# First product of a one-core transformer block: modulation columns through a product with ones, the high part of h taken from PSUM, halved first weights, another order of loads, filler products

## The chip, the core and the metric

The kernel runs on one NeuronCore of a Trainium2 chip. The metric is the device time of one execution in microseconds (us); lower is better. Five engines work side by side: TensorE (PE, matrix products; PEld is its weight load), VectorE (DVE), ScalarE (ACT), GpSimd (POOL) and SyncE (SP), which here only issues DMA transfers. All five run their own instructions strictly in the order in which the program lists them and wait for each other through semaphores.

## The reference

One layer of a hybrid block on 256 tokens of width 2048, all in float32:

```python
mod = silu(c) @ w_ada + b_ada                 # 6 x 2048: shift1, scale1, gate1, shift2, scale2, gate2
h = rms_norm(x, norm1_w) * (1 + scale1) + shift1
proj = h @ w_in                               # columns of an mLSTM group and an attention group
...                                           # mLSTM (4 heads), differential attention (8 heads)
x = x + gate1 * (concat(h_ml, o_da) @ w_out)
h = rms_norm(x, norm2_w) * (1 + scale2) + shift2
g, u = split(h @ w_gate_up)
x = x + gate2 * ((silu(g) * u) @ w_down)
```

So nothing of the first projection can start before a part of `mod` is known: for each pair of 128-row blocks of the model width, `shift1` and `scale1` of those rows. One such pair is called p (0 to 7).

## The kernel before

**Ticks.** The main stream of PE is a list of ticks. A tick multiplies 256 rows of K by 512 output columns for all 256 tokens. A float32 operand is split in a high part of type float32r and a low part (the rest), and three products stand for one: high by high, weight-low by h-high, weight-high by h-low (lines 568 to 570, `product`). A tick has 12 such products of 128x512. Its names are `wh` and `wl` (weights, high and low), `hh` and `hl` (activations), `acc('in', g, p)` (the accumulator in PSUM; `in` is the first projection, `wo` the output projection). `r` is the raw weight tile as it lands; there are three of them. ACT makes `wh` (line 211, helper `act`), DVE makes `wl` (line 181, helper `tt`), two ticks ahead of PE.

**Modulation.** `w_ada` comes in quarters of 0.5 MB (`ada`, four buffers). Some pairs are done on PE (`on_pe`): four quarters are multiplied into `gv` (line 216, 4 instructions a quarter, 8 in the trace), ACT copies `gv` to `gr`, PE transposes `gr` in two blocks into `gc` (line 220), and ACT copies four of the columns to `gsum`. POOL then adds the bias and the four parts (lines 376 and 378) and forms `gcol` = (1 + scale) x norm weight (lines 416 and 417). The other pairs are summed by DVE straight from `ada` (line 185).

**From x to h.** ACT scales x to `hx`, PE transposes it into `pt`, ACT applies `gcol` and the shift from `pt` into `hx` (128x256 twice), ACT copies that to `hh`, DVE subtracts to get `hl`.

**The order of work.** There is no scheduler: the order in the code is the order on each engine. Before the ticks stands a prelude written by hand. In the ticks, a planner (`Plan`) places steps of background work (the later h pairs, gates, attention heads, mLSTM cells) between half ticks, by estimated costs and by free PSUM banks. So an edit early in the program can move such steps much later. The background work that the text below speaks of: `gt` (the gate projection with the small weights `gwt`, line 216 from `project_gates`), `sc` (attention scores of one head, with `bmask`/`identb` products in bf16 between them), `ot` (transposes of the attention output of one group, whose high and low parts are `odh` and `odl`, inputs of the output projection), `nu`, `pp` and `L` (mLSTM), `g1rp` (spreading of the gate row).

**Loads.** All loads stand in one queue on SP. A load waits there until its buffer is free; everything behind it waits too. `small` holds the gate weights (64 KB, line 1268) and the lambda parameters.

Of the kernel before, what the change touches and what calls it, by code (L numbers as in the profile page):

```python
# [56 lines left out]
FPAIRS = 6  # L57
FSWEEPS = ((0, 2), (2, 5), (5, 8))
# [22 lines left out]
class Work:  # L81
    """Background work in steps; a step follows the one before it by at least a tick."""
# [7 lines left out]
class Plan:  # L90
    """Interleaves the steps of background work with the ticks of the main matrix products."""
# [73 lines left out]
def tile_block(ctx, tc, x, c, pos, par, w_ada, w_in, w_gt, w_out, w_gu, w_dn, out):  # L165
# [103 lines left out]
    gsum = const([P, 6, 4, 16], "gsum")  # L269
# [51 lines left out]
    def ada_use():  # L321
        s, p, q = items[ada_next[1]]
        t = ada_tiles.pop((s, p, q))
        if on_pe(s, p):
            if q == 0:
                assert plan.free > 0, "no bank"
                plan.free -= 1
                gemv[s, p] = misc(f"gv{s}_{p}")
            pg = gemv[s, p]
            for j in range(4):  # L330
                mm(pg[32 * j:32 * j + 32, :256], scol[:, q * 4 + j, :], t[:, j * 256:(j + 1) * 256], q == 0, q == 3,
                   passes=1.2, tile_position=(0, 32 * j))
            if q == 3:
                def finish():
                    yield 0
                    row = sm.tile([P, 256], F32, name=f"gr{s}_{p}", tag="gr", bufs=1)
                    act(row[:], pg[:, :256], AF.Copy)
                    plan.rel(1)
                    yield 1
                    pc = misc(f"gc{s}_{p}")  # L340
                    for j in range(2):
                        tr(pc[:, j * 128:(j + 1) * 128], row[:, j * 128:(j + 1) * 128])
                    yield 0
                    act(gsum[:, s, :, p * 2:p * 2 + 2],
                        pc[:, :256].rearrange("p (j a b) -> p a j b", j=2, b=32)[:, :, :, 0], AF.Copy)
# [22 lines left out]
    modc = const([P, 6, 16], "modc")  # L368
    badat = par_("bada").rearrange("p (s j) -> p s j", s=6)

    def modcol(s, j0, n):
        o = modc[:, s, j0:j0 + n]
        parts = [badat[:, s, j0:j0 + n]] + [gsum[:, s, i, j0:j0 + n] for i in range(4 if on_pe(s, j0 // 2) else 2)]
        if n > 2:
            parts = [badat[:, s, j0:j0 + n]] + [gsum[:, s, i, j0:j0 + n] for i in range(4)]
# [70 lines left out]
    def make_hT(i, p, late=False):  # L446
# [19 lines left out]
        if late:  # L466
            hcolumns(i, p)
# [104 lines left out]
    def products(i, half):  # L572
        """Half of a tick; the two ticks that end a group with "split" go token tile by token tile."""
# [494 lines left out]
    def turn(stage, heads):  # L1068
        """The last products of w_out and the first of w_gate_up go token tile by token tile; this is what lies between."""
# [167 lines left out]
    # how many quarters of w_ada each span of ticks takes: (first tick, last tick, items)  # L1237
# [16 lines left out]
    plan.t = 3.2  # L1254
    ada_dma(4)
    weights_dma(1)
# [5 lines left out]
    plan.free -= 1  # L1262
# [17 lines left out]
    next(h0, None)  # L1280
    plan.mark("h0_0")
    gw3 = gw.rearrange("p (k g) -> p k g", g=8)
    act(gwt[:, :, 0:8], gw3, AF.Copy)
    tt(gwt[:, :, 8:16], gw3, gwt[:, :, 0:8].bitcast(F32), ALU.subtract)
    plan.t = 21.0
# [94 lines left out]
class Lazy:  # L1380
    """A generator that is made when its first step runs; that step needs no bank before it."""
# [85 lines left out]
```

## Time and profile before

| | us |
|---|---|
| median of three runs | 1253.47 (1249.21 to 1253.92) |
| span of the profiled execution, first to last instruction | 1246.5 |
| PE busy in it | 1224.0 (98%) |
| first product of the first tick starts | 29.42 |
| first product of the third tick starts | 41.58 |

The page gives no time for the profiled execution other than its span; the median lies 6.97 us above it. A row of a timeline has the start in us, the length in us, engine, line, operation, output<-inputs, shapes and the count of instructions merged into it; in brackets stands how long the engine sat idle before it and what ended that wait. Lengths of PE rows overlap, since products are pipelined: the distance from one start to the next is the price in a stream. In the rows of a table of stretches the columns are: stretch, its length, busy time of PE, PEld, DVE, ACT and POOL (with the number of instructions), the granted PE clock as a share of full speed, the share of the 16 DMA engines, and GB/s.

### The profile page before, as it was taken

The numbers are of one execution on the slowest core, as the hardware profiler recorded it, in microseconds if no ns is written. First come the engines' busy times: TensorE is split into PE (matmuls) and PEld (weight loads), VectorE is DVE, ScalarE is ACT, GpSimd is POOL, SyncE is SP. The second block draws the span as 40 slices with busy tenths as digits, with TensorE's granted clock in tenths as the row PEclk, the third lists the DMA queues.
The fourth block names the chain that finished last, engine by engine and source line by source line (L and its number), as shares of the span: only waits on it lengthen the run. The fifth ranks groups of instructions, "written<-read, shape, count | busy, mean of one in ns | idle before, by whom it ended". The sixth has DMA issues, their size and how long they took to land.

```text
span 1246.5 us, 15450 instructions
## 1 busy us (share of the span) xinstructions
PE 1224.0 (98%) x5858; PEld 963.2 (77%) x5858; DVE 815.9 (65%) x1064; ACT 587.4 (47%) x817; POOL 112.2 (9%) x249
## 2 busy tenths in 40 slices
PE   6999999999999999999999999999999999999998
PEld 2667877667778788788888888888888878888886
DVE  2657976557667998777988986555445454545453
ACT  3654444446646644765434454434344443434332
POOL 1010221200302412011100000000000000000000
PEclk9999999989999999999999999999999999999999
DMA  8889997746755989698998856555555545646461
GB/s 332 300 299 349 343 377 282 281 151 249 256 219 194 330 331 353 264 341 302 354 352 332 309 181 218 201 176 200 188 183 197 183 169 195 220 169 223 165 251 54
DMA packets 63260, 313.84 MB, mean 252 GB/s; under 512 B 6993, under 2 KB 7377, under 8 KB 41169
## 3 DMA queue, kind: packets, MB, share of 16 engines
q1 hardware_dynamic: 63186, 312.86, 69.1%
q8 instruction: 46, 0.75, 0.2%
q14 instruction: 28, 0.23, 0.1%
HBM read 310.73 MB, written 2.10 MB: 251 GB/s over the span
## 4 chain that ended last, share of the span: by engine, by line
PE 95%; DMA 2%; DVE 1%; ACT 1%; issue 0%; SPq 0%; POOL 0%; ACTq 0%
PE gv L216 3%; PE sc L216 2%; DMA ada<-in_w_ada_dram 2%; PE acc('dn', 0)_8051 L570 2%; PE acc('dn', 0)_8051 L568 2%; PE acc('dn', 2)_8853 L570 2%; PE acc('dn', 2)_8853 L569 2%; PE acc('dn', 1)_8473 L570 2%; PE acc('dn', 1)_8473 L569 2%; PE acc('dn', 0)_8051 L569 2%; PE acc('dn', 2)_8853 L568 2%; PE acc('dn', 1)_8473 L568 2%; PE apart('dn', 3)_9234 L570 1%; PE apart('dn', 3)_9234 L569 1%; PE acc('dn', 3)_9233 L570 1%; PE acc('dn', 3)_9233 L569 1%
## 5 line engine op out<-in xcount | busy, mean ns | idle before, releaser
L181 DVE TENSOR_TENSOR wl<-r,wh 128x1024 fp32r<-128x1024 f32 x392 | 474.4, 1222 | 252.0 <-ACT wh L211 250.6
L211 ACT ACTIVATE wh<-r 128x1024 fp32r<-128x1024 f32 x392 | 410.3, 1058 | 414.6 <-DMA r<-in_w_gu_dram 64.7
L185 DVE SCALAR_TENSOR_TENSOR ada<-ada,silc 128x1024 f32<-128x1024 f32 x120 | 144.7, 1218 | 0.0
L376 POOL TENSOR_TENSOR modc<-part,gsum 128x2 f32<-128x2 f32 (+1 forms) x34 | 24.5, 722 | 396.5 <-DVE ada L185 277.7
L216 PE MATMUL gv<-ada,early 128*32 128x256 f32 x576 | 47.1, 420 | 4.6 <-DMA ada<-in_w_ada_dram 4.4
L216 PEld LDWEIGHTS gv<-ada,early 128*32 128x32 f32 x576 | 13.3, 112 | 30.5 <-issue 20.7
L568 PE MATMUL acc('dn', 0)_8051<-wh,aTh 128*128 128x512 f32 x88 | 35.9, 408 | 0.0
L378 POOL TENSOR_TENSOR modc<-modc,gsum 128x2 f32<-128x2 f32 (+1 forms) x58 | 30.9, 533 | 46.8 <-DVE ada L185 43.4
L570 PE MATMUL acc('dn', 0)_8051<-wh,aTl 128*128 128x512 f32 x88 | 34.3, 390 | 0.0
L569 PE MATMUL acc('dn', 0)_8051<-wl,aTh 128*128 128x512 f32 x88 | 34.3, 389 | 0.0
L568 PE MATMUL acc('dn', 1)_8473<-wh,aTh 128*128 128x512 f32 x88 | 34.2, 389 | 0.0
L569 PE MATMUL acc('dn', 1)_8473<-wl,aTh 128*128 128x512 f32 x88 | 34.2, 389 | 0.0
L570 PE MATMUL acc('dn', 1)_8473<-wh,aTl 128*128 128x512 f32 x88 | 34.2, 389 | 0.0
L568 PE MATMUL acc('dn', 2)_8853<-wh,aTh 128*128 128x512 f32 x88 | 34.2, 389 | 0.0
L569 PE MATMUL acc('dn', 2)_8853<-wl,aTh 128*128 128x512 f32 x88 | 34.2, 389 | 0.0
L570 PE MATMUL acc('dn', 2)_8853<-wh,aTl 128*128 128x512 f32 x88 | 34.2, 389 | 0.0
L181 DVE TENSOR_TENSOR hl<-hx,hh 128x512 fp32r<-128x512 f32 (+1 forms) x18 | 11.4, 632 | 26.7 <-ACT hh L211 26.6
L211 ACT ACTIVATE hx<-pt,modc,gcol 128x256 f32<-128x256 f32 (+1 forms) x36 | 17.4, 534 | 16.8 <-PE pt L220 11.7
L211 ACT ACTIVATE gr<-gv 128x256 f32<-128x256 f32 x18 | 6.9, 383 | 34.5 <-PE gv L216 34.5
L216 PE MATMUL sc<-kT,qT 64*128 64x128 f32 (+1 forms) x64 | 20.2, 397 | 0.0
L211 ACT ACTIVATE aTh<-at 128x512 fp32r<-128x512 f32 x22 | 11.9, 595 | 17.2 <-PE at L220 17.2
L569 PEld LDWEIGHTS acc('dn', 0)_8051<-wl,aTh 128*128 128x128 f32 x88 | 16.5, 188 | 4.2 <-issue 1.0
(987 smaller groups left out, 3041.6 us busy)
## 6 DMA issues: line engine op xcount, KB each, us to landing
ada<-in_w_ada_dram SPq DMA_DIRECT2D x192, 512.0 KB, 5.6
r<-in_w_gu_dram SPq DMA_DIRECT2D x76, 1024.0 KB, 5.1
r<-in_w_dn_dram SPq DMA_DIRECT2D x44, 1024.0 KB, 4.8
r<-in_w_in_dram SPq DMA_DIRECT2D x36, 1024.0 KB, 7.1
r<-in_w_out_dram SPq DMA_DIRECT2D x16, 1024.0 KB, 7.4
r<-in_w_in_dram SPq DMA_DIRECT2D x24, 512.0 KB, 5.9
r<-in_w_gu_dram SPq DMA_DIRECT2D x24, 512.0 KB, 5.2
x<-in_x_dram SPq DMA_DIRECT2D x4, 512.0 KB, 5.8
```

Source lines behind the costliest of these rows:

```text
L181: nc.vector.tensor_tensor(o, a, b, op=op)
L185: nc.vector.scalar_tensor_tensor(out=o, in0=a, scalar=s, in1=b, op0=op0, op1=op1, accum_out=accum)
L211: nc.scalar.activation(o, a, func, **kw)
L216: nc.tensor.matmul(o, l, r, start=start, stop=stop, **kw)
L376: nc.gpsimd.tensor_tensor(o, parts[0], parts[1], op=ALU.add)
L378: nc.gpsimd.tensor_tensor(o, o, y, op=ALU.add)
L568: nc.tensor.matmul(o, ah[:, s], wh[:, r], start=t["start"] and j == 0, stop=False)
L569: nc.tensor.matmul(o, ah[:, s], wl[:, r], start=False, stop=False)
L570: nc.tensor.matmul(o, al[:, s], wh[:, r], start=False, stop=t["stop"] and j == 1)
```

## The change

It edits the prelude and what the prelude uses.

- **Columns.** The two transposes of `gr` become two products with `gr` as the stationary operand and one column of ones as the moving one (`gc` is then the sum over the four groups of partitions). DVE adds the bias and writes `modc` straight away. `gsum` copies on ACT go, for all 18 pairs that PE does, and POOL's additions for them as well.
- **First h.** In the prelude `gcol` is formed by one DVE operation. For each half (256 columns), ACT writes `hh` straight from `pt`; DVE makes the full `hx` from `pt` by itself and then `hl`.
- **First weights.** The first tick's `wh` and `wl` are made in two halves, interleaved with the halves of `hh` and `hl` on ACT and DVE (`weights_part`).
- **Loads.** The first `r` goes behind the eighth quarter of `w_ada`; the gate weights go from the prelude into a background step (`gate_weights`).
- **Fillers.** `warm(n)` puts n bf16 products of 128x128 into a bank that nobody reads: 6 before the second pair of `gc` products, 15 behind them.

```diff
-                        tr(pc[:, j * 128:(j + 1) * 128], row[:, j * 128:(j + 1) * 128])
+                        mm(pc[:, j:j + 1], row[:, j * 128:(j + 1) * 128], ones[:, 0:1], True, True)
                     yield 0
-                    act(gsum[:, s, :, p * 2:p * 2 + 2],
-                        pc[:, :256].rearrange("p (j a b) -> p a j b", j=2, b=32)[:, :, :, 0], AF.Copy)
+                    tt(modc[:, s, p * 2:p * 2 + 2], pc[:, 0:2], badat[:, s, p * 2:p * 2 + 2], ALU.add)
...
         if late:
-            hcolumns(i, p)
+            nw = par_("n1")[:, p * 2:p * 2 + 2]
+            g = gcol[:, i, p * 2:p * 2 + 2]
+            stt(g, modc[:, s_sc, p * 2:p * 2 + 2], 1.0, nw, ALU.add, ALU.mult)
+            weights_part(0, 0)
+            for j in range(2):
...
+                act(hi[:, q], src, AF.Identity, bias=b, scale=a)
+                ts(dst, src, a, b, ALU.mult, ALU.add)
+                tt(lo[:, q], dst, hi[:, q].bitcast(F32), ALU.subtract)
+                weights_part(0, j, True)
+            plan.rel(1)
+            return
...
+    def weights_part(k, j, low=False):
...
+        if not low:
+            act(tok(hi, j), raw[:, o:o + 512], AF.Copy)
+            return
+        tt(tok(lo, j), raw[:, o:o + 512], tok(hi, j).bitcast(F32), ALU.subtract)
+        if j == 0:
+            weights_part(k, 1)
...
+    def warm(n):
+        for _ in range(n):
+            mm(idle_bank[:, :128], identb[:], cmask[:], True, True, passes=0)
...
     ada_dma(4)
-    weights_dma(1)
...
-    nc.sync.dma_start(gw, w_gt[:, :])
-    nc.sync.dma_start(lamt, par[:, NPAR - 256:])
     weights_dma(1)
...
     while "ada0_0" not in plan.done:
         plan.next_half()
         plan.run(force=True)
+        warm(WARM0 if "ada0_0" not in plan.done else WARM1)
...
+    def gate_weights():
+        yield 0
+        nc.sync.dma_start(gw, w_gt[:, :])
+        nc.sync.dma_start(lamt, par[:, NPAR - 256:])
+        yield 0
+        yield 0
+        gw3 = gw.rearrange("p (k g) -> p k g", g=8)
+        act(gwt[:, :, 0:8], gw3, AF.Copy)
+        tt(gwt[:, :, 8:16], gw3, gwt[:, :, 0:8].bitcast(F32), ALU.subtract)
+
+    plan.add("gw", gate_weights())
```

**The start, queue of SP.** Before, behind the eighth quarter of `w_ada` (`ada_0_3`; in these names the first number is the pair p, the second the quarter):

```order
L315 DMA ada_0_3_216<-in_w_ada_dram 128x1024
L1268 DMA small<-in_w_gt_dram 128x128
L1269 DMA small<-in_par_dram 128x256
L514 DMA r_220<-in_w_in_dram 128x1024
L315 DMA ada_1_0_227<-in_w_ada_dram 128x1024
```

Now, from the same quarter on:

```order
L319 DMA ada_0_3_215<-in_w_ada_dram 128x1024
L531 DMA r_217<-in_w_in_dram 128x1024
L531 DMA r_241<-in_w_in_dram 128x1024
L319 DMA ada_1_0_243<-in_w_ada_dram 128x1024
L319 DMA ada_1_1_245<-in_w_ada_dram 128x1024
L531 DMA r_247<-in_w_in_dram 128x1024
L319 DMA ada_1_2_249<-in_w_ada_dram 128x1024
L319 DMA ada_1_3_251<-in_w_ada_dram 128x1024
L531 DMA r_304<-in_w_in_dram 128x1024
L531 DMA r_306<-in_w_in_dram 128x1024
L531 DMA r_308<-in_w_in_dram 128x1024
L319 DMA ada_1_0_315<-in_w_ada_dram 128x1024
```

The gate weights (`small`) are the next rows behind these: eleven large loads have come between the eighth quarter and them. `r_304`, `r_306` and `r_308` each take the buffer of one of the first three ticks and wait until DVE has made that tick's `wl`.

**The start, PE around the second tick.** Before, `gt` stood in the middle of the second tick:

```order
L570 MATMUL acc('in', 2, 0)_333<-wh_281,hl_0_197 128x512
L216 MATMUL gt_342<-hh_0_196,gwt 16x256
L216 MATMUL gt_342<-hl_0_197,gwt 16x256
L216 MATMUL gt_342<-hh_0_196,gwt 16x256
L216 MATMUL gt_342<-hl_0_197,gwt 16x256
L216 MATMUL gv_1_297<-ada_1_3_250,early 32x256 x4
```

Now it stands between the second tick and the third:

```order
L613 MATMUL acc('in', 2, 0)_342<-wh_296,hl_0_196 128x512
L217 MATMUL gv_1_310<-ada_1_2_249,early 32x256 x4
L217 MATMUL gv_1_310<-ada_1_3_251,early 32x256 x4
L217 MATMUL gt_377<-hh_0_195,gwt 16x256
L217 MATMUL gt_377<-hl_0_196,gwt 16x256
L217 MATMUL gt_377<-hh_0_195,gwt 16x256
L217 MATMUL gt_377<-hl_0_196,gwt 16x256
L611 MATMUL acc('in', 6, 0)_390<-wh_298,hh_0_195 128x512
```

All work on PE behind `gt` now waits for `gwt`, whose raw data is the `small` load above.

**The attention scores, PE.** Before, the scores of two heads stood back to back (here the end of one and the start of the next):

```order
L216 MATMUL sc_0_2301<-bmask,identb 128x128
L216 MATMUL sc_1_2302<-kT_2230,qT_2057 128x256
L216 LDWEIGHTS identb
L216 MATMUL sc_1_2302<-bmask,identb 128x128
L216 MATMUL sc_0_2311<-kT_2230,qT_2057 128x128
L216 LDWEIGHTS identb
L216 MATMUL sc_0_2311<-bmask,identb 128x128
```

Now there are six products or more between any two heads:

```order
L217 MATMUL sc_1_2236<-bmask,identb 128x128
L611 MATMUL acc('in', 7, 4)_2224<-wh_2134,hh_2_1191 128x512
L612 MATMUL acc('in', 7, 4)_2224<-wl_2156,hh_2_1191 128x512
L613 MATMUL acc('in', 7, 4)_2224<-wh_2134,hl_2_1192 128x512
L611 MATMUL acc('in', 7, 4)_2224<-wh_2134,hh_2_1191 128x512
L612 MATMUL acc('in', 7, 4)_2224<-wl_2156,hh_2_1191 128x512
L613 MATMUL acc('in', 7, 4)_2224<-wh_2134,hl_2_1192 128x512
L217 MATMUL sc_0_2259<-kT_2215,qT_2042 128x128
```

The planner, fed with other costs, has spread the heads. There were two such pairs of heads before and there are none now.

**The output projection, PE.** Before, six products, `g1rp` and `pp` stood between `ot` and the first product that needs its `odh`:

```order
L220 MATMUL ot_1_3684<-ident,o_3438 128x128 x4
L216 MATMUL g1rp_3696<-g1rd_3648,ones 128x512
L568 MATMUL acc('wo', 0)_3650<-wh_3566,odh_3147 128x512
...
L570 MATMUL acc('wo', 0)_3650<-wh_3566,odl_3148 128x512
L220 MATMUL pp_3715<-ident,ml_2894 128x128 x3
L568 MATMUL acc('wo', 0)_3650<-wh_3631,odh_3711 128x512
```

Now that product follows at once:

```order
L613 MATMUL acc('wo', 0)_3584<-wh_3525,odl_3146 128x512
L221 MATMUL ot_0_3659<-ident,o_3213 128x128 x4
L221 MATMUL ot_1_3660<-ident,o_3213 128x128 x4
L611 MATMUL acc('wo', 0)_3584<-wh_3572,odh_3672 128x512
L612 MATMUL acc('wo', 0)_3584<-wl_3591,odh_3672 128x512
L613 MATMUL acc('wo', 0)_3584<-wh_3572,odl_3673 128x512
```

On DVE, the queue from the eviction of the last `in` accumulator to `odl` is now: that eviction, `wl`, four small operations, `ada`, `wl`, two for `ml`, `ada`, `o` (which `ot` transposes), `ada`, `ada`, `odl`. The rest of the order, the whole feed-forward part among it, is the same but for a few single steps.

More of the change, by code (lines that the diff above doesn't have):

```diff
@@ L57 @@
 FPAIRS = 6
+WARM0, WARM1 = 3, 12
 FSWEEPS = ((0, 2), (2, 5), (5, 8))
@@ L268, in tile_block @@
     nc.gpsimd.memset(scol, 0.0)
-    gsum = const([P, 6, 4, 16], "gsum")
+    gsum = const([P, 6, 2, 16], "gsum")
     nc.gpsimd.memset(gsum[:], 0.0)
@@ L296, in tile_block @@
         act(tok(silc[q // 2], q % 2), pq[:], AF.Silu)
+    modc = const([P, 6, 16], "modc")
+    badat = par_("bada").rearrange("p (s j) -> p s j", s=6)
     items = []
@@ L366, in ada_idle @@
             ada_dma(1)
-    modc = const([P, 6, 16], "modc")
-    badat = par_("bada").rearrange("p (s j) -> p s j", s=6)
     def modcol(s, j0, n):
         o = modc[:, s, j0:j0 + n]
-        parts = [badat[:, s, j0:j0 + n]] + [gsum[:, s, i, j0:j0 + n] for i in range(4 if on_pe(s, j0 // 2) else 2)]
-        if n > 2:
-            parts = [badat[:, s, j0:j0 + n]] + [gsum[:, s, i, j0:j0 + n] for i in range(4)]
+        kinds = {on_pe(s, j // 2) for j in range(j0, j0 + n)}
+        assert len(kinds) == 1
+        if True in kinds:
+            return o
+        parts = [badat[:, s, j0:j0 + n]] + [gsum[:, s, i, j0:j0 + n] for i in range(2)]
         nc.gpsimd.tensor_tensor(o, parts[0], parts[1], op=ALU.add)
@@ L466, in make_hT @@
         if late:
-            hcolumns(i, p)
+            nw = par_("n1")[:, p * 2:p * 2 + 2]
[3 more added lines that the diff above has]
+            for j in range(2):
+                col = p * 2 + j
+                q = slice(half * 512 + j * 256, half * 512 + j * 256 + 256)
+                src, dst = pt[:, j * 256:(j + 1) * 256], full[:, j * 256:(j + 1) * 256]
+                b, a = modc[:, s_sh, col:col + 1], gcol[:, i, col:col + 1]
+                act(hi[:, q], src, AF.Identity, bias=b, scale=a)
[4 more added lines that the diff above has]
+            return
         for j in range(2):
@@ L544, in weights_lo @@
                 del raws[first]
+    def weights_part(k, j, low=False):
+        first, idx, n = chunk_of[k]
+        raw, o = raws[first], idx * 1024 + j * 512
+        if k not in his:
+            his[k] = wp.tile([P, 1024], F32R, name=f"wh{k}", tag="hi", bufs=NHL + HI_AHEAD)
+            wtiles[k] = (his[k], wp.tile([P, 1024], F32R, name=f"wl{k}", tag="lo", bufs=NHL))
+        hi, lo = wtiles[k]
+        if not low:
[4 more added lines that the diff above has]
+            weights_part(k, 1)
+        else:
+            his.pop(k)
+            state["hi"] += 1
+            state["hl"] += 1
+            state["live"] -= 1
+            del raws[first]
     apart = {}
+    def warm(n):
+        for _ in range(n):
+            mm(idle_bank[:, :128], identb[:], cmask[:], True, True, passes=0)
     def acc_tile(acc, k):
@@ L1261, in tile_block @@
     h0 = make_hT(0, 0, late=True)
-    plan.free -= 1
+    plan.free -= 2
+    idle_bank = misc("idle")
     for n in range(4):
@@ L1272, in tile_block @@
         ada_use()
-        ada_dma(1)
-        plan.next_half()
-        plan.run(force=True)
+        if n < 3:
+            plan.next_half()
+            plan.run(force=True)
     weights_dma(1)
+    ada_dma(2)
+    weights_dma(1)
+    ada_dma(2)
     while "ada0_0" not in plan.done:
@@ L1279, in tile_block @@
         plan.run(force=True)
+        warm(WARM0 if "ada0_0" not in plan.done else WARM1)
     next(h0, None)
     plan.mark("h0_0")
[L1282 to L1285, printed above, removed]
+    plan.rel(1)
+    plan.t = 19.5
     plan.v = plan.a = 3.0
+    def gate_weights():
[8 more added lines that the diff above has]
+    plan.add("gw", gate_weights())
     for p in range(1, 8):
@@ L1290, in tile_block @@
     for p0, p1 in ((0, 1), (1, 2), (2, 4), (4, 8)):
-        plan.add(f"gates{p0}", project_gates(p0, p1), [f"h0_{p}" for p in range(p0, p1)])
-    plan.add("tables", small_tables())
+        plan.add(f"gates{p0}", project_gates(p0, p1), [f"h0_{p}" for p in range(p0, p1)] + ["gw"])
+    plan.add("tables", small_tables(), ["gw"])
     plan.add("gates", gates(), ["gates4"])
```

## The prediction

> **What bounds the kernel now.** The page first: span, busy time, and the granted PE clock in 40 slices of 31 us.
>
> ```profile
> span 1246.5 us, 15450 instructions
> PE 1224.0 (98%) x5858; PEld 963.2 (77%) x5858; DVE 815.9 (65%) x1064; ACT 587.4 (47%) x817; POOL 112.2 (9%) x249
> PEclk9999999989999999999999999999999999999999
> ```
>
> PE is the bound nearly everywhere, so time can be won only where PE stands still or runs at a lower clock. One slice of PEclk, 249 to 280 us, shows an 8; what is low in the first two slices hides in the rounding. Then the timeline of PE at the start, up to the third tick.
>
> ```profile
> 22.56 0.87 PE L216 MATMUL gv<-ada,early 128*32 128x256 f32 x8
> 24.00 0.44 PE L220 MATMUL gc<-ident,gr 128*128 128x128 f32 x2 [0.57 <-ACT gr L211]
> 26.41 1.05 PE L216 MATMUL gv<-ada,early 128*32 128x256 f32 x8 [1.96 <-DMA ada<-in_w_ada_dram]
> 29.42 0.80 PE L568 MATMUL acc('in', 0, 0)_304<-wh,hh 128*128 128x512 f32 x1 [1.96 <-ACT wh L211]
> 30.68 0.80 PE L569 MATMUL acc('in', 0, 0)_304<-wl,hh 128*128 128x512 f32 x1 [0.46 <-DVE wl L181]
> 31.27 0.63 PE L570 MATMUL acc('in', 0, 0)_304<-wh,hl 128*128 128x512 f32 x1
> 31.70 0.63 PE L568 MATMUL acc('in', 0, 0)_304<-wh,hh 128*128 128x512 f32 x1
> 41.58 0.40 PE L568 MATMUL acc('in', 6, 0)_376<-wh,hh 128*128 128x512 f32 x1
> 41.81 0.39 PE L569 MATMUL acc('in', 6, 0)_376<-wl,hh 128*128 128x512 f32 x1
> ```
>
> From the end of the eighth quarter's products (23.43) to the second product of the first tick (30.68) PE does almost nothing. And products start 0.43 us apart at 31.3, 0.23 apart at 41.6: the clock was at half. Next, the engines that PE waits for, and the clock by stretches.
>
> ```profile
> 23.57 0.38 ACT L211 ACTIVATE gr<-gv 128x256 f32<-128x256 f32 x1 [5.44 <-PE gv L216]
> 26.54 1.02 ACT L211 ACTIVATE hx<-pt,modc,gcol 128x256 f32<-128x256 f32 x2 [1.88 <-POOL gcol L417]
> 27.59 0.63 ACT L211 ACTIVATE hh<-hx 128x512 fp32r<-128x512 f32 x1
> 28.32 1.99 ACT L211 ACTIVATE wh<-r 128x1024 fp32r<-128x1024 f32 x2
> 29.40 2.36 DVE L181 TENSOR_TENSOR wl<-r,wh 128x1024 fp32r<-128x1024 f32 x2 [0.25 <-ACT wh L211]
> ...
> 26.00:27.00 1.00, 0.59 (x8) 0.21 (x8) 0.00 (x0) 0.46 (x1) 0.42 (x3) 0.75 1.04 418
> 36.00:37.00 1.00, 1.00 (x7) 0.44 (x9) 0.00 (x0) 0.00 (x0) 0.00 (x0) 0.63 0.86 213
> 264.00:266.00 2.00, 2.00 (x9) 1.19 (x8) 2.00 (x5) 0.94 (x1) 0.00 (x0) 0.86 0.28 115
> 272.00:274.00 2.00, 2.00 (x10) 1.65 (x9) 0.28 (x1) 0.51 (x1) 0.00 (x0) 0.94 0.89 250
> ```
>
> One chain after `gr`: POOL until 26.5, `hx`, `hh`, `wh`, then the whole `wl`. The means 0.75 and 0.63 put the fall of the clock to half at 26.5 and its return at 36.7; 0.86 and 0.94 put a second fall at 265.4 and a return at 272.2, where PE never idled but ran only scores (`sc`) of two heads back to back. That second stretch of 6.8 us at half clock costs 3.4 us.
>
> **The change, part by part.** *Loads.* SP and the landings:
>
> ```profile
> 13.20 4.87 SPq L315 DMA_DIRECT2D ada<-in_w_ada_dram  x4
> ...
> DMA to landing us min/median/max: 4.0/5.4/10.6
> ...
> L211 ACT ACTIVATE gwt<-small x1: 293/293/293, 28.1 to 28.1; 128x128 fp32r<-128x128 f32 x1
> L181 DVE TENSOR_TENSOR gwt<-small,gwt x1: 284/284/284, 28.9 to 28.9; 128x128 fp32r<-128x128 f32 x1
> ```
>
> The eighth quarter of `w_ada` is issued at the end of that SP row, about 17.7, since its buffer is free only then. Taking `r` out of its way cannot help beyond the shortest landing of a 0.5 MB tile (4.0, row of `r`): it lands at 21.75 and its products start at 21.8 instead of 22.56, 0.8 us earlier, and end at 22.9 at 1.05 a set.
>
> *Columns and fillers.* `gr` ends at 23.3. The six fillers stand ahead of `gc` on PE. No filler stream is in the trace; the nearest bf16 row stands between scores at half clock:
>
> ```profile
> 266.01 0.29 PE L216 MATMUL sc<-bmask,identb 128*128 128x128 bf16 x1
> 266.23 1.22 PE L216 MATMUL sc<-kT,qT 64*128 64x256 f32 x2
> ```
>
> Start to start 0.22, so six cost at most 1.3 and end by 24.2; at least nothing, where they run while ACT copies. I take 23.9, the middle. `gc` 0.45 (24.00 row), two small operations on DVE at under 0.3 each (`gwt` row) against 2.5 us of POOL: `gcol` at 24.9. Half of `hx` from `pt` on ACT is 0.51 (half of 1.02): the first half of `hh` is there at 25.4. DVE then needs a 256-column and a 512-column subtraction, a quarter and a half of 1.2 (`wl` row): `wl`'s first half at 26.4, its second, by the same prices, at 27.8. The second product could thus start at 26.4, against 30.68. On PE fifteen fillers (at most 3.3) and one `gv` set (1.05) stand ahead: 25.8 at the earliest, 28.7 at the latest; I take 27. With the clock up by then (the fillers leave no gap over 1 us), a tick is 12 x 0.23 = 2.8: first tick to 29.8, `gv` 0.6, second tick to 33.2, two `gv` sets to 34.4.
>
> *Gate weights.* Then `gt` waits. Its data land behind eleven tiles (the eighth quarter to `gt`'s load in SP's queue); at 418 GB/s (row 26.00:27.00) a tile takes 1.25 to 1.28: 21.75 + 11 x 1.28 = 35.8, 0.2 for the 64 KB, 0.6 for ACT and DVE: 36.7. SP reaches that load in time only if the third tick's `wl` is done by 30.5, which frees the last buffer ahead of it; DVE has 27.8 + 2 x 1.2 = 30.2. PE so idles 2.3 us there, and this pin, not the chain above, sets the third tick. The four `gt` products:
>
> ```profile
> 38.96 0.28 PE L216 MATMUL gt<-hh,gwt 128*16 128x256 f32 x1
> ...
> 39.52 0.64 PE L216 MATMUL gv<-ada,early 128*32 128x256 f32 x8
> ```
>
> 0.56, so the third tick starts at 37.3 instead of 41.58. **Start: -4.3**, from -5.0 (a pin 0.7 earlier) to -3. The work ahead of the third tick is the same in both. PE's next wait, for the second h pair (its row stands at rival 1), stays: ACT's order there is unchanged.
>
> *Scores.* The pairs of heads are gone: at least six products, 1.4 us at 0.23, lie between the scores of any two heads now, and single heads did not lower the clock in any other slice. **-3.4**, from -3.4 to 0.
>
> *Ones.* A product with one moving column still loads 128 columns of weights, twice as float32. The nearest row is a 16-column product (`gz`), beside the transposes and what follows them:
>
> ```profile
> L884 PEld LDWEIGHTS gz<-ident,early x2: 136/137/138, 217.5 to 217.5; 16*128 16x128 f32 x2
> ...
> 322.83 0.38 PE L220 MATMUL gc<-ident,gr 128*128 128x128 f32 x2
> 323.14 0.64 PE L216 MATMUL gv<-ada,early 128*32 128x256 f32 x8
> ```
>
> Four loads at 0.137 are 0.55, less what is pulled ahead, say 0.45, against 0.31: +0.14, 16 times in PE's stream: **+2.2**, from 0 to 3.8. The Trainium skill, "TensorE: Matmul & The Clock Gate", LDWEIGHTS, says that a load's time goes by its columns (128 / 1.2 ns, 107 ns): by it an estimate of 0.43, +1.9 in all. This trace's loads are longer, so the row decides. The DVE additions now wait for `gc` with a later tick's `wl` behind them: 1.2 us in two ticks of 2.8, covered; uncovered it would cost up to 1.2 at a place.
>
> *Output projection.* `odh` and `odl` now have no cover:
>
> ```profile
> 412.04 1.04 PE L220 MATMUL ot<-ident,o 128*128 128x128 f32 x8
> 412.91 1.02 PE L216 MATMUL g1rp<-g1rd,ones 128*128 128x512 f32 x2
> 416.78 0.50 PE L570 MATMUL acc('wo', 0)_3650<-wh,odl 128*128 128x512 f32 x1 [0.66 <-DVE odl L185]
> ...
> 406.83 1.22 DVE L181 TENSOR_TENSOR proj<-proj,acc('in', 11, 6)_3545 128x1024 f32<-128x1024 f32 x1 [1.51 <-PE acc('in', 11, 6)_3545 L570]
> 409.72 1.21 DVE L181 TENSOR_TENSOR o<-o,of 128x1024 f32<-128x1024 f32 x1
> 415.99 1.39 DVE L185 SCALAR_TENSOR_TENSOR odl<-ot,subc,odh 128x512 fp32r<-128x512 f32 x2
> ...
> 413.23 1.27 ACT L211 ACTIVATE odh<-ot,subc 128x512 fp32r<-128x512 f32 x2
> ```
>
> From the eviction at 406.83 on, DVE's new queue to the end of `o` is six wide operations (6 x 1.15 to 1.2) and six small ones (an estimate of 1.3): 8.3. PE's is the old 5.2 to `ot` plus six products (1.4) and `g1rp` (0.9): 7.5. So `ot` waits 0.8, then 0.75 for `odh` (0.63 and a semaphore), then about 0.9 for `odl`, which stands behind two `ada` sums: 2.4 instead of 0.66. **+1.7**, from 0 (other queues shorter) to 3.9.
>
> Sum: -4.3 - 3.4 + 2.2 + 1.7 = -3.8. The page has no time of the profiled execution but its span; 6.97 us lie between that and the median, and I keep them: span 1242.7, time **1249.7**. A measurement of this kernel can tell about 0.5% (6.3 us) from no change.
>
> **The rivals.** (1) *The gate wait cools PE.* The 2.3 us before `gt`, after two low-use `gv` sets, lets the clock fall for one or two steps of 3.4 us (10.2 and 6.8 seen here are three and two): +1.7 to +3.4, 1251.4 to 1253.1. For: the clock fell at 26.5 after gaps of 0.57 and 1.96. Against:
>
> ```profile
> 68.53 0.29 PE L216 MATMUL gt<-hh,gwt 128*16 128x256 f32 x1 [2.26 <-ACT hh L211]
> ```
>
> no fall came after this gap. 23%. The Trainium skill, same page, "Why this matters for your kernels", allows gaps up to about 3 us; by it this rival is nil, but the fall at 26.5, with no gap of 2 us before it, disagrees.
>
> (2) *The late costs are hidden.* The ones' loads go under the products before them and `odl` comes in time: 1253.47 - 7.7 = 1245.8. For: PE's loads overlap elsewhere; against: the `gz` row. 22%.
>
> (3) *The output projection cools PE; slower.* If `odl` comes as late behind `ot` as before (416.7 against 413.1, 3.6), PE idles 4 us: 3.3 more than before instead of 1.7, and past some 2.3 us of idling the clock falls as at 265: +3.4. 1249.7 + 1.6 + 3.4 = 1254.7. 7%.
>
> (4) *The fillers do not do what they are for.* At half clock to 36.7 as before, two ticks from 27 on take 24 x 0.43, three `gv` sets 3.2, `gt` 1.1: third tick at 41.6, nothing won at the start: 1254.0. 6%.
>
> **How the numbers follow.** Forecast 42%, the rivals 23, 22, 7 and 6. The range leaves out (3) and (4): up to 1253.3, the end of (1), and down to 1244.8, (2) with the earlier pin and 0.3 of spread. Faster by over 0.5% (below 1247.2): all of (2) and one in seven of the forecast, where the ones are cheap: 0.28. Slower by over 0.5% (above 1259.7) takes (3) and (4) together: 0.02. The rest, 0.70, is within.
>
> **What would show it.** Right: `gv` of the eighth quarter at 21.8; the first product at 27 and 0.23 us steps; an idle of about 2.3 us at `gt` ended by DVE `gwt`; the third tick at 37.3; no slice under 9 near 260; `gc` pairs of 0.45 to the next start; 2.4 us of idling around `ot`. Wrong: a third tick before 36 or after 39, steps of 0.43 behind `gt`, a low clock among the scores, or idling of PE at places that had none.

## The result, and the profile after

The changed kernel takes 1257.65 us (median of six runs, 1255.79 to 1259.29) against 1252.86 for the kernel before (six runs): a ratio of 1.0044, 95% interval 1.0028 to 1.0061, or +5.5 us (3.5 to 7.6) by that ratio; the two medians lie 4.8 apart. The forecast was 1249.7; the result lies outside the range, on the slower side. Wherever a run lists its span, of either kernel, time less span is 1.7 to 1.8 us. The profiled execution of the changed kernel took 1255.79.

The page of the changed kernel:

```profile
span 1254.1 us, 15533 instructions
PE 1227.7 (98%) x5915; PEld 970.2 (77%) x5915; DVE 818.6 (65%) x1087; ACT 584.9 (47%) x799; POOL 95.3 (8%) x201
PEclk8999999999999999999999999999999999999999
```

The slice with an 8 is now the first, not the one around 260. The timeline of PE at the start:

```profile
22.15 1.08 PE L217 MATMUL gv<-ada,early 128*32 128x256 f32 x8
23.16 0.82 PE L217 MATMUL idle<-cmask,identb 128*128 128x128 bf16 x6
24.67 1.76 PE L217 MATMUL idle<-cmask,identb 128*128 128x128 bf16 x15
27.06 1.08 PE L217 MATMUL gv<-ada,early 128*32 128x256 f32 x8 [0.63 <-DMA ada<-in_w_ada_dram]
28.07 0.80 PE L611 MATMUL acc('in', 0, 0)_317<-wh,hh 128*128 128x512 f32 x1
28.67 0.63 PE L612 MATMUL acc('in', 0, 0)_317<-wl,hh 128*128 128x512 f32 x1
29.09 0.63 PE L613 MATMUL acc('in', 0, 0)_317<-wh,hl 128*128 128x512 f32 x1
...
35.67 1.07 PE L217 MATMUL gv<-ada,early 128*32 128x256 f32 x16
40.19 0.28 PE L217 MATMUL gt<-hh,gwt 128*16 128x256 f32 x1 [3.45 <-DVE posf L638]
...
40.66 0.51 PE L611 MATMUL acc('in', 6, 0)_390<-wh,hh 128*128 128x512 f32 x1
40.96 0.63 PE L612 MATMUL acc('in', 6, 0)_390<-wl,hh 128*128 128x512 f32 x1
41.39 0.63 PE L613 MATMUL acc('in', 6, 0)_390<-wh,hl 128*128 128x512 f32 x1
```

PE has done the second tick by 35.67, when in the kernel before it was still in the first. But it then stands 3.45 us before `gt`, and the products behind it come to start 0.43 apart: half clock. The bracket names `posf`, a small DVE operation; what `gt` reads is `gwt`, which DVE finishes just ahead of it, at 40.04. Where `gwt` comes from, on SP, ACT and DVE:

```profile
28.89 3.29 SPq L531 DMA_DIRECT2D r<-in_w_in_dram  x3
32.27 0.38 SPq L319 DMA_DIRECT2D ada<-in_w_ada_dram  x1
32.71 0.42 SPq L1333 DMA_DIRECT2D small<-in_w_gt_dram  x1
...
29.51 1.06 ACT L212 ACTIVATE wh<-r 128x1024 fp32r<-128x1024 f32 x1 [1.72 <-DMA r<-in_w_in_dram]
39.41 0.31 ACT L212 ACTIVATE gwt<-small 128x128 fp32r<-128x128 f32 x1 [4.32 <-DMA small<-in_w_gt_dram]
...
30.60 1.23 DVE L182 TENSOR_TENSOR wl<-r,wh 128x1024 fp32r<-128x1024 f32 x1 [0.63 <-ACT wh L212]
...
39.75 0.29 DVE L182 TENSOR_TENSOR gwt<-small,gwt 128x128 fp32r<-128x128 f32 x1 [3.40 <-ACT gwt L212]
```

The third tick's `wl` ends at 31.83, SP gives out the last of three weight loads then, reaches the gate weights at 32.71, and ACT has them at 39.4 only. Stretches of the changed kernel (their clock stands ahead of the last two columns):

```profile
40.80:44.20 3.40, 3.40 (x10) 2.61 (x9) 2.69 (x10) 1.29 (x3) 0.00 (x0) 0.50 0.91 341
416.20:419.70 3.50, 3.49 (x12) 2.35 (x11) 3.50 (x7) 2.32 (x3) 2.25 (x4) 0.51 1.03 419
250.00:300.00 50.00, 50.00 (x270) 35.35 (x269) 34.82 (x74) 30.12 (x63) 3.55 (x4) 1.00 0.51 178
300.00:372.00 72.00, 72.00 (x435) 53.28 (x434) 46.28 (x102) 42.36 (x105) 11.01 (x42) 1.00 0.58 208
```

The clock falls behind the wait at `gt` and at the output projection, and nowhere among the scores. The output projection, on PE, DVE and POOL:

```profile
415.99 1.70 PE L221 MATMUL ot<-ident,o 128*128 128x128 f32 x8 [2.90 <-DVE o L182]
...
405.52 1.22 DVE L182 TENSOR_TENSOR proj<-proj,acc('in', 11, 6)_3510 128x1024 f32<-128x1024 f32 x1 [1.36 <-PE acc('in', 11, 6)_3510 L613]
414.62 1.23 DVE L182 TENSOR_TENSOR o<-o,of 128x1024 f32<-128x1024 f32 x1 [2.06 <-POOL of L393]
...
408.65 1.10 POOL L390 TENSOR_TENSOR of<-of 128x8 f32<-128x8 f32 x1 [21.99 <-DVE of L193]
409.83 1.07 POOL L391 TENSOR_TENSOR of<-of 128x8 f32<-128x8 f32 x1
...
411.55 1.06 POOL L390 TENSOR_TENSOR of<-of 128x8 f32<-128x8 f32 x1
...
414.38 0.20 POOL L393 TENSOR_TENSOR of<-of 128x8 f32<-128x8 f32 x1
```

DVE itself waits there, for twelve small operations on POOL. In the kernel before these began ahead of the eviction (406.83) and ended before `o` came up (409.72):

```profile
404.88 0.20 POOL L387 TENSOR_TENSOR of<-of 128x8 f32<-128x8 f32 x1 [3.20 <-DVE of L192]
...
407.99 0.72 POOL L390 TENSOR_TENSOR of<-of 128x8 f32<-128x8 f32 x1
```

Last, a wait in the feed-forward part (`at`: transposes of the activated part `fp`), after and, in the second fence, the first of them before:

```profile
698.46 1.09 PE L221 MATMUL at<-ident,fp 128*128 128x128 f32 x8 [1.44 <-DVE fp L182]
734.11 1.09 PE L221 MATMUL at<-ident,fp 128*128 128x128 f32 x8 [0.59 <-DVE fp L182]
```

```profile
694.82 1.03 PE L220 MATMUL at<-ident,fp 128*128 128x128 f32 x8
```

The planner put both of these twelve products earlier than before, where `fp` isn't ready yet.

**A balance of each trace.** To compare traces I split the time from the third tick's first product to the end of the last product in three: idling of PE (gaps over 0.15 us), half of the time at half clock (less the idling in it), and the rest, which is what PE's work would take at full clock. For the kernel before: 41.58 + 6.52 + 3.41 + 1190.29 = 1241.8, the end of its last product.

| kernel | third tick | idle | half clock | rest | span |
|---|---|---|---|---|---|
| before | 41.58 | 6.52 | 3.41 | 1190.29 | 1246.5 |
| before, second profile (before_again) | 40.58 | 6.28 | 10.21 | 1189.61 | 1251.4 |
| after | 40.66 | 10.56 | 3.41 | 1194.77 | 1254.1 |
| after, second profile (after_again) | 41.74 | 11.22 | 5.94 | 1195.00 | 1258.6 |
| gw_early | 38.72 | 10.49 | 3.25 | 1194.69 | 1251.8 |
| late_tr | 42.19 | 11.28 | 6.11 | 1191.54 | 1255.8 |
| old_order | 39.10 | 6.31 | 6.78 | 1192.82 | 1249.7 |
| new_order | 39.78 | 10.28 | 3.41 | 1191.65 | 1249.8 |
| b_spread | 40.55 | 6.47 | 1.69 | 1190.77 | 1244.2 |
| ones_alone | 40.83 | 7.61 | 3.39 | 1193.70 | 1250.2 |
| best | 39.56 | 6.28 | 3.41 | 1191.11 | 1245.0 |
| best_nofill | 39.27 | 6.28 | 1.71 | 1191.06 | 1243.0 |
| best_whole | 41.81 | 6.27 | 3.41 | 1190.36 | 1246.5 |
| best_dense | 37.85 | 7.76 | 3.41 | 1190.41 | 1244.1 |

In the two pairs of profiles of one kernel the third tick differs by up to 1.1, idle and rest by up to 0.7, half clock by up to 6.8. Idle holds 5.6 that every trace has (2.7 at the second h pair, 2.9 at the first `gu` products); what is above is 0.9 before and 4.9 after, 2.9 of it at `ot` and 2.0 at `at`.

### The profile page after: what moved, and what is told of

Same layout as the page of the kernel before. It is cut to its first block, busy times and chain, and to the rows that moved or that the text cites. A ratio compares the mean times of both kernels' runs of the same rounds, so it can differ in the third digit from the quotient of the medians.

```text
span 1254.1 us, 15533 instructions
## 1 busy us (share of the span) xinstructions
PE 1227.7 (98%) x5915; PEld 970.2 (77%) x5915; DVE 818.6 (65%) x1087; ACT 584.9 (47%) x799; POOL 95.3 (8%) x201
## 4 chain that ended last, share of the span: by engine, by line
PE 89%; DMA 5%; DVE 4%; issue 1%; ACT 1%; POOL 0%; SPq 0%; ACTq 0%; DVEq 0%
PE gv L217 3%; PE sc L217 2%; DMA r<-in_w_gu_dram 2%; PE acc('dn', 0)_8032 L613 2%; PE acc('dn', 0)_8032 L612 2%; PE acc('dn', 2)_8832 L612 2%; PE acc('dn', 1)_8452 L613 2%; PE acc('dn', 1)_8452 L612 2%; PE acc('dn', 2)_8832 L613 2%; PE acc('dn', 2)_8832 L611 2%; PE acc('dn', 0)_8032 L611 2%; PE acc('dn', 1)_8452 L611 2%; DMA ada<-in_w_ada_dram 2%; DVE wl L182 1%; DVE ada L186 1%
## 5 line engine op out<-in xcount | busy, mean ns | idle before, releaser
L182 DVE TENSOR_TENSOR wl<-r,wh 128x1024 fp32r<-128x1024 f32 (+1 forms) x393 | 475.4, 1219 | 249.8 <-ACT wh L212 248.6
L212 ACT ACTIVATE wh<-r 128x1024 fp32r<-128x1024 f32 (+1 forms) x393 | 411.1, 1056 | 411.1 <-DMA r<-in_w_gu_dram 58.5
L611 PE MATMUL acc('dn', 0)_8032<-wh,aTh 128*128 128x512 f32 x88 | 35.9, 408 | 0.0
L613 PE MATMUL acc('dn', 0)_8032<-wh,aTl 128*128 128x512 f32 x88 | 34.3, 390 | 0.0
L612 PE MATMUL acc('dn', 0)_8032<-wl,aTh 128*128 128x512 f32 x88 | 34.3, 389 | 0.0
L611 PE MATMUL acc('dn', 1)_8452<-wh,aTh 128*128 128x512 f32 x88 | 34.2, 389 | 0.0
L612 PE MATMUL acc('dn', 1)_8452<-wl,aTh 128*128 128x512 f32 x88 | 34.2, 389 | 0.0
L613 PE MATMUL acc('dn', 1)_8452<-wh,aTl 128*128 128x512 f32 x88 | 34.2, 389 | 0.0
L611 PE MATMUL acc('dn', 2)_8832<-wh,aTh 128*128 128x512 f32 x88 | 34.2, 389 | 0.0
L612 PE MATMUL acc('dn', 2)_8832<-wl,aTh 128*128 128x512 f32 x88 | 34.2, 389 | 0.0
L613 PE MATMUL acc('dn', 2)_8832<-wh,aTl 128*128 128x512 f32 x88 | 34.2, 389 | 0.0
```

The costliest lines, as they stand in the source:

```text
L182: nc.vector.tensor_tensor(o, a, b, op=op)
L212: nc.scalar.activation(o, a, func, **kw)
L611: nc.tensor.matmul(o, ah[:, s], wh[:, r], start=t["start"] and j == 0, stop=False)
L612: nc.tensor.matmul(o, ah[:, s], wl[:, r], start=False, stop=False)
L613: nc.tensor.matmul(o, al[:, s], wh[:, r], start=False, stop=t["stop"] and j == 1)
```

## The experiments

All ratios are to the kernel before on the same chip. To hold the order of later work fixed, some kernels replace the planner in the ticks by a table of its decisions, recorded from the one or the other kernel:

```diff
-    for i, t in enumerate(ticks):
-        plan.next_half()
...
+    for e in SCRIPT.split():
+        if e[0] == "s":
+            w = next(w for w in plan.works if w.name == e[2:])
...
+SCRIPT = """
+h0 h1 h2 l0 l1 l2 w3 w4 w5 u8 d12 p0.0 u9 d13 p0.1 f0.done h3
```

In the table p is a half tick, s a step of background work, u the use of a quarter of `w_ada`, d and w are loads, h and l a tick's `wh` and `wl`.

**gw_early: the gate weights first.**

```diff
     weights_dma(1)
+    nc.sync.dma_start(gw, w_gt[:, :])
     for n in range(4):
...
     def gate_weights():
         yield 0
-        nc.sync.dma_start(gw, w_gt[:, :])
```

> The changed kernel (1257.65), with one line moved: the load of the gate weights stands behind the first weight tile again, and everything else, the order of all later work too, is as in the changed kernel. Theory A (the late gate weights cost the start 3.45 us of idling at gt and then 1.7 us of a low clock): gt does not wait, the third tick starts at 37 instead of 40.66 with steps of 0.23, and the time falls by 5.2 to 1252.5; the idling at ot (2.9) and at the two at blocks (1.4, 0.6) stays. Rival B (the start is bound by transfers, so what is won at gt is given back at the next wait, for the second h pair at 67): the idle there grows from 2.3 to over 5, and the time stays at 1257 to 1258.

1253.69 (ratio 1.0030, 1.0014 to 1.0046).

```profile
28.12 1.08 PE L217 MATMUL gv<-ada,early 128*32 128x256 f32 x8 [2.12 <-DMA ada<-in_w_ada_dram]
38.25 0.28 PE L217 MATMUL gt<-hh,gwt 128*16 128x256 f32 x1 [0.63 <-DVE posf L638]
38.72 0.40 PE L611 MATMUL acc('in', 6, 0)_390<-wh,hh 128*128 128x512 f32 x1
38.95 0.40 PE L612 MATMUL acc('in', 6, 0)_390<-wl,hh 128*128 128x512 f32 x1
```

The wait at `gt` shrinks to 0.63 and no clock falls behind it: 1.94 at the third tick and 1.7 of clock, 3.6 in all at that place. The profile keeps 2.3 of it (spans 1254.1 and 1251.8), since the fall behind `ot` lasts 6.8 us here (413.5 to 420.3) instead of 3.4. The two ratios differ by 1.8 us, with 2 of uncertainty on each, against 5.2 expected: theory A is shown for the wait and the clock at this place, its price in time is not. The idle at the second h pair stays at 2.69, so rival B is out. The third tick comes at 38.7 and not 37. The next `gv` set, which stands ahead of the first product, waits 2.12 for its tile, and the clock is back at 31.2 only; which of the two costs the 1.7 isn't shown (best, below, has no such `gv` set there, and its third tick comes at 39.56).

**old_order and new_order: the order of later work.** old_order is the changed kernel's start and columns, gate weights loaded early, in the recorded order of the kernel before; new_order is the kernel before in the order of the changed one.

> The changed kernel's start, columns and fillers with the gate weights loaded early, and all background steps in the order of the kernel before (written out as a table). Theory C (the planner's new order costs 3.9 at ot, idle and clock, and 2.9 at the at blocks, and saves 3.4 among the scores): beside gw_early, no idle at ot over 0.7, none at at, the clock falls among the scores again; 3.4 faster than gw_early, by theory A at 1249.1. Rival D (the order costs nothing on the whole; the loss lies in the start and the columns alone): within 1 of gw_early.

> The kernel before (1252.86), its start and its columns by transposes untouched, with only the background steps in the order that the changed kernel gave them. Theory C: no low clock among the scores (-3.4), idling of about 3 us at ot with a low clock behind it (+3.9) and at the at blocks (+2.9): 1256.3. Rival D: 1252.9, within 1 of the kernel before.

old_order takes 1251.86 (1.0005, 0.9987 to 1.0022), new_order 1252.91 (1.0015, 0.9999 to 1.0030). new_order, on PE and by stretches:

```profile
412.13 1.76 PE L220 MATMUL ot<-ident,o 128*128 128x128 f32 x8 [2.90 <-DVE o L181]
...
412.30:415.80 3.50, 3.50 (x12) 2.41 (x12) 3.50 (x7) 2.32 (x3) 2.29 (x4) 0.51 1.05 425
250.00:372.00 122.00, 122.00 (x693) 87.85 (x692) 77.95 (x161) 72.35 (x172) 16.40 (x55) 1.00 0.55 199
```

The order alone brings the whole idle at `ot`, the fall behind it and the idle at `at` (1.8) into the kernel before, and takes the falls among the scores out. old_order waits 0.69 near `ot`, as the kernel before does, with no fall behind it and nothing at `at`, and has a fall of 6.8 us among the scores, at 364. So theory C is right about each place. Its sum for new_order was 3.4 too high, and on the whole the time is what rival D gave: 1.9 us for the order, -0.1 to 3.8. What the order costs at `ot` and `at`, 6.8 by the rows, and what it saves among the scores nearly cancel; the saving is larger than the first profile showed, as before_again and b_spread show.

**late_tr and ones_alone: the price of a ones product.** late_tr is the changed kernel with transposes for the 16 later pairs, ones_alone is b_spread (below) with ones for them; its edit:

```diff
                     for j in range(2):
-                        tr(pc[:, j * 128:(j + 1) * 128], row[:, j * 128:(j + 1) * 128])
+                        if first:
+                            tr(pc[:, j * 128:(j + 1) * 128], row[:, j * 128:(j + 1) * 128])
+                        else:
+                            mm(pc[:, j:j + 1], row[:, j * 128:(j + 1) * 128], ones[:, 0:1], True, True)
```

> The changed kernel with the 16 later pairs of columns by transposes again (and ACT's copies and POOL's sums for them), in the same order of steps. Theory E (16 pairs of gc take 0.20 us more of PE each as ones products than as transposes): 2.9 to 3.2 faster, 1254.6. Rival F (PE's weight loads go under other work, or the later chain over ACT and POOL costs as much): within 1 of 1257.65.

> b_spread (the kernel before with its heads taken apart, 1246.6) with the 16 later columns by ones products and nothing else. Theory E (ones cost PE 0.20 us more at each of 16 places): the rest of PE's work 1193.8 to 1194 against 1190.8, and 3 slower than b_spread, 1249.7. Rival F (the loads go under other work): within 1 of b_spread.

late_tr takes 1253.96 (1.0036, 1.0018 to 1.0053): 1.0 better than after by the ratios, which can't tell 3 from 0, but its rest is 3.2 lower. ones_alone takes 1250.17 (0.9987, 0.9972 to 1.0002): 0.0030, or 3.8 us, over b_spread, and its rest is 2.9 higher (its profile also has a wait of 1.35 at 609 that no other has). The same pair in b_spread and in ones_alone:

```profile
96.71 0.38 PE L220 MATMUL gc<-ident,gr 128*128 128x128 f32 x2
96.85 0.48 PE L568 MATMUL acc('in', 1, 1)_874<-wh,hh 128*128 128x512 f32 x1
```

```profile
97.68 0.50 PE L216 MATMUL gc<-ones,gr 128*128 128x1 f32 x4
98.04 0.48 PE L578 MATMUL acc('in', 1, 1)_862<-wh,hh 128*128 128x512 f32 x1
```

0.36 to the next start in ones_alone against 0.14 in b_spread. Theory E holds, by the rests of two pairs of profiles and by one of the two times: about 3 us.

**before_again, after_again and b_spread: the clock among the scores.** The first two are second profiles of the kernels as they are. b_spread is the kernel before, its order recorded, with the second head's scores six products later at two places.

```diff
-s:at0 s:at1 s:at2 p66.0 l68 s:at1 s:at2 p66.1 h69 s:at1 p67.0
+s:at0 s:at1 p66.0 l68 s:at1 s:at2 p66.1 h69 s:at1 s:at2 p67.0
```

> The kernel before once more, unchanged, for a second profile of it. Its profiled execution had a span of 1246.5, some 4 below the spans of its usual executions (time less 1.7). Theory M (the usual execution spends more time at half clock than the one that was profiled, since the scores lower the clock at both pairs of heads or for longer): 10 us or more at half clock after the third tick (6.8 then), most of it among the scores; idling 6.5 and the rest of PE's work 1190 as then. Rival N (the difference is in waits for transfers): idling or rest larger by 3 to 4, the clock as then.

> The changed kernel once more, unchanged, for a second profile of it. Theory: idle at gt 2 to 3.5, at ot 2.9, at the at blocks 2.0, rest of PE's work 1194.8 as in the first, all within 0.5 but gt; only the stretches at half clock and the start change, by windows of 3.41 us. Rival (the idling at ot and at is chance): it is gone or twice as long.

> The kernel before with one thing changed: at the two places where the scores of two heads stood back to back, the second head's scores go six products later. Theory G (scores back to back lower the clock): no low clock among the scores, 250 to 372 us, and 1.7 to 3.4 faster than before, 1249.1 to 1250.8. Rival H (the stretches at half clock come and go by the position of fixed windows of 3.41 us, and are only moved to another place): as many us at half clock after the third tick as in the kernel before (6.8), and the same time, 1252.5.

Stretches of before_again, then the same stretches of b_spread:

```profile
266.20:273.00 6.80, 6.80 (x17) 4.52 (x17) 3.99 (x11) 2.08 (x8) 1.32 (x2) 0.50 0.12 19
365.20:372.00 6.80, 6.80 (x18) 4.37 (x18) 1.68 (x6) 0.00 (x0) 0.41 (x2) 0.50 0.37 145
```

```profile
266.20:273.00 6.80, 6.80 (x34) 4.74 (x33) 4.12 (x12) 3.51 (x11) 1.32 (x2) 1.00 0.07 11
365.20:372.00 6.80, 6.80 (x31) 5.39 (x32) 4.59 (x9) 4.53 (x13) 1.11 (x1) 1.00 0.01 5
```

before_again (1253.09) loses 3.4 at both places where heads stood back to back, and 1.7 at each of two others; the first profile, span 1246.5, had lost 3.4 at one place. Of the 64 times of the kernel before in the experiments, 22 lie from 1247.1 to 1250.1 and 42 from 1251.2 to 1255.3: the first profile (1246.5 + 1.7) is one of the quicker third. b_spread loses it at neither and takes 1246.62 (0.9957, 0.9942 to 0.9972): 5.4 faster than the kernel before, by an edit that moves two sets of scores. On PE's queue nothing else differs between the two kernels, so theory G is right and its price too small. Rival H is out, with one fall of 3.4 us behind the third tick; M is right. after_again repeats idle at `ot` (2.90 ahead of it), at `at` (1.41 and 0.33) and rest within 0.3; at `gt` it waits 4.20.

**best, best_nofill, best_whole, best_dense: the start alone.** All four have the changed kernel's start, gate weights early, transposes for the later columns, and b_spread's order with the next `gv` set behind the first six products. best_nofill sets both filler counts to 0; best_whole makes the first weights whole, behind h; best_dense uses wider fillers, and some of them earlier:

```diff
-WARM0, WARM1 = 3, 12
+WARM0, WARM1 = 1, 4
...
-            mm(idle_bank[:, :128], identb[:], cmask[:], True, True, passes=0)
+            mm(idle_bank.rearrange("p (a b) -> p a b", a=4), identb[:], cmask[:].unsqueeze(1).to_broadcast([P, 4, P]), True, True, passes=0)
...
     for n in range(4):
         ada_use()
         if n < 3:
+            warm(2)
```

> The changed kernel's start with the gate weights loaded early, the next gv set moved from ahead of the first product to behind the first six, the 16 later columns by transposes again, and the steps in the order of the kernel before with its two pairs of heads taken apart. Theory, all terms together: first product at 27 or before (no wait for the transfer of the next w_ada quarter ahead of it), third tick at 37 to 38 against 41.6, idling after it as in the kernel before (6.3), the rest of PE's work as in the kernel before (1190.3): 5.7 faster than before, 1246.8. Rival B (the start is bound by transfers, what is won is idled away at 67): 1250 to 1252.

> The kernel best without the 21 filler products. Theory I (the fillers bring the clock back earlier): the clock is up one or two windows of 3.41 us later than in best, the third tick 1 to 2 us later, the time 1.7 slower. Rival J (the fillers do not do what they are for; the clock returns when products run, filler or not): the same within 1.

> The kernel best with the first tick's weights made whole, behind both halves of h (as one wh and one wl of 1024 columns). Theory K (the halves shorten the chain to the first two products): the first product 0.6 and the second 0.8 to 1.5 us later than in best, the third tick 0.8 later. Rival L (transfers and the clock set the third tick): the third tick within 0.3 of best.

> best with other fillers: bf16 products with 512 moving columns (15 in all), two behind each of the fourth to seventh gv sets and ahead of the second gc, five behind it, in place of 21 with 128 columns. Theory O (the clock goes by how many columns PE streams in a window, and the 128-column fillers are mostly weight loads): the clock is at full speed at the first product, at 27, or a window later, third tick at 36 to 37.5 against 39.6, 2 to 3.5 faster than best, 1242. Rival J (no filler brings the clock back before the products do, or they delay the chain as much): third tick at 39 to 41, within 1 of best or slower.

best takes 1245.02 (0.9938, 0.9921 to 0.9954), best_nofill 1244.51 (0.9943, 0.9927 to 0.9960), best_dense 1242.38 (0.9922, 0.9897 to 0.9948); best_whole, run once, 1248.28. The fillers of the change do nothing that can be measured here (rival J); a gain of 1.7 lies within the uncertainty of the times, but the third tick without them comes at 39.27, not later than the 39.56 with them. Stretches of best and, below, of best_dense:

```profile
24.00:27.40 3.40, 3.40 (x30) 3.22 (x26) 1.04 (x4) 2.37 (x5) 0.00 (x0) 0.50 1.00 369
27.40:30.80 3.40, 2.99 (x10) 1.65 (x13) 3.37 (x7) 1.44 (x3) 0.00 (x0) 0.50 1.03 417
```

```profile
23.40:26.80 3.40, 2.84 (x19) 1.13 (x19) 0.24 (x3) 1.51 (x4) 0.00 (x0) 1.00 0.99 338
26.80:30.20 3.40, 2.25 (x15) 1.21 (x14) 3.33 (x8) 2.19 (x4) 0.00 (x0) 1.00 1.01 405
```

best keeps PE busy all through 24.0 to 27.4 and stays at half clock to 34.2. best_dense holds the full clock from 19.8 on, and its third tick stands at 37.85 against 39.56; the two products that open it:

```profile
37.85 0.39 PE L620 MATMUL acc('in', 6, 0)_387<-wh,hh 128*128 128x512 f32 x1
38.08 0.39 PE L621 MATMUL acc('in', 6, 0)_387<-wl,hh 128*128 128x512 f32 x1
```

It then waits 1.46 for a `w_ada` tile at 40.7, so little of the 1.7 is left in its profile (spans 1244.1 and 1245.0). The difference between the two ratios, 0.0016 or 2 us, is within their uncertainty. So these fillers keep the clock up, and a gain in time isn't shown. Theory O, that the width of the fillers does it, isn't separated from their places: best's clock fell at 20.6, behind a window with 1.85 us of idling, and best_dense has fillers from 17.8 on in that idling. In best_whole the first product comes at 29.10 against 27.03 and waits for `wh`; the clock also came back later there (36.6 against 34.2), so of its 2.25 at the third tick only a part is the halves'. best, best_nofill and best_dense are faster than both kernels; most of that is b_spread's order, which alone gives 0.9957. The high part of h from PSUM, the ones columns of the first pair and the new place of the first `r` have no run of their own.

## Why the prediction was wrong

**The start, -4.3: the step that failed is "SP reaches that load in time only if the third tick's `wl` is done by 30.5, which frees the last buffer ahead of it; DVE has 27.8 + 2 x 1.2 = 30.2".** DVE was free by then, but ACT's `wh` for that tick waited for its `r` until 29.51, `wl` ended at 31.83, and SP's loads of `r`, each waiting for a buffer, held the gate weights back to 32.71. The eighth quarter landed as forecast (its `gv` at 22.15 against 21.8), but the loads behind it did not come at the 418 GB/s that the sum took for all eleven: from 30 to 36 us, in steps of 2, they moved 268, 289 and 238. PE stood 3.45 and not 2.3, and the clock fell for 3.4 us: rival (1), 23%. What had been held against that rival, a gap of 2.26 without a fall, was luck of that execution: in 11 of the 14 profiles the clock fell behind the same gap (last section). The start came out at -0.9 + 1.7 = +0.8 between the two first profiles. Even the -0.9 is no gain that is shown: in the four profiles with the start of the kernel before (before, before_again, b_spread, ones_alone) the third tick comes at 40.55 to 41.58, mean 40.9; in the three with the changed start as it is (after, after_again, late_tr) at 40.66 to 42.19, mean 41.5.

**The first product at 27 with steps of 0.23.** It came at 28.07, with steps of 0.43 up to 30.6. The `gv` set ahead of it was priced by its length, not by its tile, which landed third behind the eighth quarter. That the fillers leave no gap over 1 us was true and did not matter: the clock had fallen at 20.3, before they ran, and came back at 30.55. This is rival (4), 6%, in its mechanism, with an earlier return than its 36.7; by best_nofill the fillers are worth nothing that can be measured.

**Scores, -3.4.** The mechanism was right (no fall from 250 to 372); the size was too small: measured alone (b_spread) it is 5.4, from 3.5 to 7.3. The profiled execution was 5 below the median; against the second profile it had been spared 6.8 us of lost clock. The 6.97 us from span to median, kept as a constant, were 1.7 of constant and about 5 of such falls. That error helped the forecast by luck: its span, 1242.7, is 11.4 off the 1254.1 of the first profile after, its time only 8.0 off.

**Ones, +2.2.** +3.0 (0.36 against 0.14 in the stream; 2.9 and 3.2 in the rests); within the bounds given.

**Output projection, +1.7.** +2.2 of idle and +1.7 of clock: 3.9, the upper end. The sum "8.3 on DVE, 7.5 on PE" left out POOL: `of` starts 3.1 behind the eviction (408.65 against 405.52), takes 5.9 us instead of 3.8, and holds `o` back by 2.06. This is what rival (3), 7%, had come out of it, a long wait and a fall of the clock, but at another place: it had PE wait 4 us for `odl`, and PE waited 2.9 for `o`.

**What was not in the sum.** "A few single steps" in the feed-forward part were not in the sum, that is, they were put at nothing, without a reason. They cost 2.0 of idle at `at`, and between the same products of the two traces the distance grows by 1.97 and 0.96 there: 2.9.

The sum by rows: 0.8 - 3.4 + 3.0 + 3.9 + 2.9 = 7.2, of 7.6 between the two profiled spans. Of the 11.4 by which the span was off, 5.1 lie in the start, 2.9 in the feed-forward part, 2.2 in the output projection and 0.8 in the ones; 0.4 stay without a place. With the scores at 5.4, as b_spread has them, and the third tick at the means above (+0.6 in place of -0.9) the sum is 6.7; the measured +5.5 (3.5 to 7.6) contains it. The range failed since two rivals and an uncosted edit came together, all on one side; it had been put together as if one of them would happen at a time.

## What to carry to other kernels

When an edit changes a planner's inputs, treat the new order as a change of its own: record both orders and run each with the other's edits, for here the new order cost about 7 us at two places and saved about 5 at a third, and the time of new_order alone shows neither. A load that is moved behind others in a queue with full buffers waits for the last buffer's release, and not only for the bytes ahead of it. Before a profiled span is used as the base of a forecast, compare it with the spans of several executions, and count the stretches at half clock in it.

## What the runs showed of the hardware

**The clock moves on a grid that differs from one execution to the next.** In the changed kernel's trace it returned at 44.20 and fell next at 416.25: 372.05, 109 times 3.413; every stretch at half clock between the third tick and the last product lasts one or two of these windows, 3.41 or 6.83. The Trainium skill, "TensorE: Matmul & The Clock Gate", What's actually happening, gives such a free-running window of 3413 ns; the trace agrees. So the same idle may or may not cost: the 2.26 and 0.43 at the second h pair lowered the clock in 11 of 14 profiles, and in neither first profile of the two kernels. Where the grid cuts decides it. In the eleven, 1.90 to 2.70 of that idle lay in one window; in the other three the grid split it into 1.18 and 1.51 (before), 1.01 and 1.70 (after), 1.76 and 0.93 (gw_early). Over all 14 traces, from 36 us to the last product and with gaps over 0.02 us counted, the clock fell at the end of each of the 23 windows at full clock with more than 1.78 us of idle, of two of the five with 1.63 to 1.76, and of none with less, but for the four falls among the scores, where PE had no idle.

**A window in which PE is busy is not enough to bring the clock back.** Products of 128 columns, with a weight load each, and those of `gc` filled 24.0 to 27.4 in best and left it at half; so did the window from 23.4 to 26.8 in after_again, which has no idle either. In best_dense the clock, once up at 19.8, stayed up with 2.84 and 2.25 busy of 3.40; that is holding it, not bringing it back. What the gate counts stays open.

**POOL slows under DVE.** Three of the twelve `of` operations took 1.06 to 1.10 and nine 0.20; the three ran each beside a 1024-wide DVE operation on two operands in SBUF (`ada` from 408.47 and 411.31, `wl` from 409.62); while DVE waited, from 412.6 on, all took 0.20. The Trainium skill, "GPSIMD Engine Reference", Specifications, says that POOL's way to SBUF is shared with VectorE and contended by its instructions with two SBUF inputs; the trace agrees.
